# Resident matmul pieces stored with reversed columns and read last to first, in a hybrid decoder layer

## The chip, the cores and the metric

The kernel runs on one core of a Trainium2 chip. Its five engines work side by side, each through its own list of instructions: TensorE (PE, matrix products, with its weight loads shown apart as PEld), VectorE (DVE), ScalarE (ACT), GpSimd (POOL) and SyncE (SP, which here only starts DMAs). The metric is the time on the device in microseconds (us), from launch to end. Beside the runs there is one profiled execution, from which all rows of the profile come.

## The reference

One layer of a decoder is computed for a prompt of 2048 tokens and for 8 x 4 sample tokens, width 1024, all in fp32. After a mixer of recurrent heads come a projection, a cross-attention over 256 memory tokens and a feed-forward part, each with its norms:

```python
def decoder_layer(x, s_gla, s_ssm, conv_buf, mk, mv, lw):
    m, s_gla, s_ssm, conv_buf = mixer(rmsnorm(x, lw['ln_mix_pre']), s_gla, s_ssm, conv_buf, lw)
    h = x + rmsnorm(m, lw['ln_mix_post'])
    a = cross_attend(rmsnorm(h, lw['ln_xa_pre']), mk, mv, lw['w_xq'], lw['w_xo'])
    h = h + rmsnorm(a, lw['ln_xa_post'])
    hf = rmsnorm(h, lw['ln_ffn_pre'])
    f = (jax.nn.silu(hf @ lw['w_gate']) * (hf @ lw['w_up'])) @ lw['w_down']
    h = h + rmsnorm(f, lw['ln_ffn_post'])
    return h, s_gla, s_ssm, conv_buf
```

The mixer ends with a product by `w_out`; the feed-forward width is 2816. The change concerns the products of the prompt from `w_out` on.

## The kernel before

**Two parts.** The first, up to some 838 us, computes the mixer block by block (512 tokens each). The second, which the change touches, runs the large products of the prompt as nine passes: `o` (projection out of the mixer), `s` (scores) and `v` (values), each with 8 units; three passes `g` (gate and up, one for each block of 3, 3 and 2 pairs of token tiles, 22 units each); three passes `d` (down, over 3, 4 and 4 groups of the inner dimension, 8 units each). That is 114 units.

**Products.** A unit is a product of matrices halved in both dimensions, made from seven smaller products in place of eight (the scheme of Strassen and Winograd): sums of quadrants are formed beforehand (`S1` to `S4` and the like), and the seven results are added into four quadrants. In each of the seven, the stationary operand (the weights loaded into TensorE) belongs to the unit and changes with it, and the moving operand stays resident in SBUF for a whole pass. The resident operands of a pass are its seven *pieces*, tiles `r0` to `r6` and, where a piece has four slices of 512 columns, also `e0` to `e6`. A slice is what one matmul streams: 512 columns in the passes `o`, `s`, `v` and `d`; 384, 384 and 272 in the three passes `g`.

**fp32 by three matmuls.** Every operand is split into a high part, rounded to the reduced format fp32r that TensorE takes, and a low part, the rest. `three` (lines 135 to 137) then issues high x high, high x low and low x high into the same bank of PSUM; line 136 takes the low part of the moving operand. The banks of the passes are accA (products 0, 2, 4 and 6 of a unit), accB (product 1) and accC (products 3 and 5).

**How pieces are made.** `pieces_w` (weights) and `pieces_g` (activations) list, for each of the seven pieces, one or more parts. A part's `load(t)` starts a DMA on SP's queue into a staged tile `st` (lines 1778 and 1795) and gives back a view `v` of the staged columns and a function from a resident tile to the place of these columns in it. `Pieces.larger` writes the high part there on ScalarE (line 1739); `smaller` writes staged minus high as the low part (line 1743), on VectorE, or for the second parts of the first `d` pass on GpSimd. The function is applied to the tile of the high part and to that of the low part alike. `Pieces.moving(i, k)` gives the slices that the matmuls of product `i`, step `k` stream.

**Order.** The order of the work is written out by hand: the loop over `order` issues the products of a unit, evacuates its banks, splits the next units' stationary operands (lines 1650, 1668 and 1670) and takes one step of the pieces that come next. The pieces of a pass are made during the last unit of the pass before and its own first unit; before a product's matmuls are issued, the loop completes its piece (`while i not in held[n].full`). `pin` keeps each engine's instructions in the order in which they were traced.

Of the kernel before, what the change touches and what calls it, by code (L numbers as in the profile page):

```python
# [42 lines left out]
def hymba_kernel(ctx: ExitStack, tc: tile.TileContext, a: dict, o: dict, dbg: dict | None = None):  # L43
    nc = tc.nc
# [1656 lines left out]
    class Pieces:  # L1701
# [61 lines left out]

        def moving(self, i, k):
            if self.wide:
                return [r[k // 2][:, k % 2 * 512:(k % 2 + 1) * 512] for r in self.at[i]]
            return [r[:, k * self.w:(k + 1) * self.w] for r in self.at[i]]

    def pieces_w(k, w, t, u0, n):

        wd = lambda h, e: w[h, u0:u0 + n, :, e * 512:(e + 1) * 512].rearrange("u p c -> p u c")
        ts = lambda i: t[i][:, u0:u0 + n]
        srcs = [wd(0, 0), wd(0, 1), ts(1), ts(0), ts(2), wd(1, 1), ts(3)]

        def part(i, k0, k1):
            def load(t):
                v = t[:, 0:(k1 - k0) * 512]
                nc.sync.dma_start(out=v.rearrange("p (k c) -> p k c", c=512), in_=srcs[i][:, k0:k1])
                return v, lambda r: r[k0 // 2] if n == 4 else r[:, k0 * 512:k1 * 512]
            return load  # L1780
        cuts = [(0, 2), (2, n)] if n > 2 else [(0, n)]
        return Pieces(k, [[part(i, *c) for c in cuts] for i in range(7)], 512, 3, n == 4)

    def pieces_g(k, blk):
        js = BLOCKS[blk]
        n = len(js)
        ws = NS // 2 if blk == len(BLOCKS) - 1 else 0
        w = n * P + ws

        by = lambda r: r[:, 0:4 * w].rearrange("p (k w) -> p k w", w=w)  # L1790

        def part(i, n0, n1):
            def load(t):
                v = t[:, 0:(n1 - n0) * 512]
                nc.sync.dma_start(out=v.rearrange("p (j c) -> p j c", c=512), in_=xp[i, js[n0]:js[n0] + n1 - n0].rearrange("j p c -> p j c"))
                return v.rearrange("p (j k c) -> p k j c", k=4, c=P), lambda r: by(r)[:, :, n0 * P:n1 * P].rearrange("p k (j c) -> p k j c", c=P)
            return load

        def sample_part(i):
            def load(t):  # L1800
                v = t[:, 0:4 * ws]
                nc.sync.dma_start(out=v, in_=xps[i])
                return v.rearrange("p (k c) -> p k c", c=ws), lambda r: by(r)[:, :, n * P:w]
            return load
        cuts = [(0, 2), (2, n)] if n > 2 else [(0, n)]
        return Pieces(k, [[part(i, *c) for c in cuts] + ([sample_part(i)] if ws else []) for i in range(7)], w, 3)
# [324 lines left out]
    def pieces_of(k):  # L2131
        kind, i, _ = passes[k]
        if kind == "g":
            return pieces_g(k, i)
        if kind == "d":
            return pieces_w(k, a["w_down"], wT, *PARTS[i])
        return pieces_w(k, *{"o": (a["w_out"], wX[0]), "s": (flat2(wqk), wX[1]), "v": (flat2(wvo), wX[2])}[kind], 0, 4)
# [134 lines left out]
    for e, (n, i) in enumerate(order):  # L2272
        k, g, left = work[n]
        kind, b, gs = passes[k]
        if i == 0:
# [6 lines left out]
            w = now.w  # L2282
# [29 lines left out]
        w = held[n].w  # L2312
# [23 lines left out]
        p = coming if work[cur][2] == 1 else now if begins[cur] else None  # L2336
# [117 lines left out]
```

## Time and profile before

| | |
|---|---|
| median of 3 runs | 2814.31 us (2811.24 to 2816.92) |
| the profiled execution, its own time | 2820.75 us |
| its span, first to last instruction | 2819.0 us |
| mean granted clock of TensorE | 0.991 |
| TensorE busy | 2729.5 us, 97% of the span |
| VectorE busy | 2079.1 us, 74% |
| ScalarE busy | 1472.8 us, 52% |
| GpSimd busy | 536.8 us, 19% |
| moved by DMA | 512.17 MB |

A row of a group of instructions names the line of the kernel, the engine, the operation, the tiles (out<-in), the shape and the count; then busy time in us and the mean of one in ns; then the idle time just before them and what ended it. The chain of waits follows the work that ended last back to the start. TensorE's durations overlap (the next matmul starts before the last one's modelled end), so its pace is read from the starts in the timeline, whose columns are start in us, duration in us, engine and line.

### The profile page before, as it was taken

The numbers are of one execution on the slowest core, as the hardware profiler recorded it, in microseconds if no ns is written. First come the engines' busy times: TensorE is split into PE (matmuls) and PEld (weight loads), VectorE is DVE, ScalarE is ACT, GpSimd is POOL, SyncE is SP. The second block draws the span as 40 slices with busy tenths as digits, with TensorE's granted clock in tenths as the row PEclk, the third lists the DMA queues.
The fourth block names the chain that finished last, engine by engine and source line by source line (L and its number), as shares of the span: only waits on it lengthen the run. The fifth ranks groups of instructions, "written<-read, shape, count | busy, mean of one in ns | idle before, by whom it ended". The sixth has DMA issues, their size and how long they took to land.

```text
span 2819.0 us, 41809 instructions
## 1 busy us (share of the span) xinstructions
PE 2729.5 (97%) x15207; PEld 2367.6 (84%) x15207; DVE 2079.1 (74%) x3831; ACT 1472.8 (52%) x2921; POOL 536.8 (19%) x722
## 2 busy tenths in 40 slices
PE   8999999999998999999899999999999999999998
PEld 8987888788886878878799888899998998788786
DVE  7676677776757787677888787667678878574776
ACT  5545554554546787777755434434445555353432
POOL 2142332321321321015321210001000001000011
PEclk9999999999999999999999999999999999999999
DMA  7345435343266785468864567775234436464765
GB/s 255 113 142 188 148 106 160 118 131 90 83 215 226 282 291 223 146 189 254 263 222 179 177 237 243 253 254 178 98 137 171 156 120 209 168 219 99 239 152 132
DMA packets 151102, 512.17 MB, mean 182 GB/s; under 512 B 18176, under 2 KB 29488, under 8 KB 137328
## 3 DMA queue, kind: packets, MB, share of 16 engines
q1 hardware_dynamic: 94560, 331.81, 36.0%
q0 software_dynamic: 44240, 152.82, 16.8%
q10 hardware_dynamic: 12096, 24.86, 2.7%
q8 instruction: 120, 1.97, 0.3%
q14 instruction: 86, 0.70, 0.1%
HBM read 365.76 MB, written 143.67 MB: 181 GB/s over the span
## 4 chain that ended last, share of the span: by engine, by line
PE 75%; DVE 13%; ACT 5%; DMA 3%; issue 3%; POOL 1%; DVEq 0%; ACTq 0%; SPq 0%; POOLq 0%
PE accA L135 9%; PE accA L136 9%; PE accA L137 9%; PE accC L135 5%; PE accC L136 5%; PE accC L137 5%; PE acc L135 5%; PE acc L136 5%; PE acc L137 5%; PE accB L135 2%; PE accB L137 2%; PE accB L136 2%; DVE s L1670 2%; DVE sum L1650 2%; ACT r L1739 1%
## 5 line engine op out<-in xcount | busy, mean ns | idle before, releaser
L135 PE MATMUL accA<-r,s 128*128 128x512 f32 (+2 forms) x1792 | 637.2, 356 | 19.0 <-ACT r L1739 7.2
L137 PE MATMUL accA<-r,s 128*128 128x512 f32 (+2 forms) x1792 | 629.1, 351 | 2.9 <-DVE s L1670 2.8
L136 PE MATMUL accA<-r,s 128*128 128x384 f32 (+2 forms) x1472 | 502.7, 342 | 2.4 <-DVE r L1743 2.4
L135 PEld LDWEIGHTS accA<-r,s 128*128 128x128 f32 x1792 | 339.2, 189 | 70.9 <-ACT r L1739 11.0
L1668 ACT ACTIVATE s<-sum 128x512 fp32r<-128x512 f32 (+1 forms) x456 | 282.5, 620 | 218.9 <-DVE sum L1650 105.0
L137 PEld LDWEIGHTS accA<-r,s 128*128 128x128 f32 x1792 | 339.7, 190 | 33.2 <-DVE s L1670 4.0
L135 PE MATMUL accC<-r,s 128*128 128x512 f32 (+2 forms) x896 | 318.8, 356 | 9.2 <-ACT s L1668 3.2
L1670 DVE TENSOR_TENSOR s<-sum,s 128x512 fp32r<-128x512 f32 (+1 forms) x456 | 306.8, 679 | 20.1 <-ACT s L1668 19.8
L137 PE MATMUL accC<-r,s 128*128 128x512 f32 (+2 forms) x896 | 314.3, 351 | 0.0
L136 PEld LDWEIGHTS accA<-r,s 128*128 128x128 f32 x1472 | 279.0, 190 | 19.2 <-DVE r L1743 3.6
L1670 DVE TENSOR_TENSOR s<-raw,s 128x512 fp32r<-128x512 f32 (+1 forms) x342 | 233.7, 683 | 52.0 <-ACT s L1668 50.9
L136 PE MATMUL accC<-r,s 128*128 128x384 f32 (+2 forms) x736 | 251.3, 341 | 0.5 <-DVE r L1743 0.5
L1668 ACT ACTIVATE s<-raw 128x512 fp32r<-128x512 f32 (+1 forms) x342 | 213.3, 624 | 72.1 <-PE accC L137 49.8
L129 ACT ACTIVATE whi<-wraw 128x1024 fp32r<-128x1024 f32 (+2 forms) x140 | 128.9, 934 | 184.2 <-PE acc L136 104.5
L135 PEld LDWEIGHTS accC<-r,s 128*128 128x128 f32 x896 | 169.8, 189 | 37.2 <-ACT s L1668 7.8
L130 DVE TENSOR_TENSOR wlo<-wraw,whi 128x1024 fp32r<-128x1024 f32 (+2 forms) x140 | 156.2, 1127 | 48.0 <-ACT whi L129 47.3
L137 PEld LDWEIGHTS accC<-r,s 128*128 128x128 f32 x896 | 169.7, 189 | 14.9 <-DVE s L1670 0.2
L143 POOL TENSOR_TENSOR rs<-ms,nhalf 128x1 f32<-128x1 f32 (+4 forms) x125 | 111.0, 889 | 360.3 <-DVE ms L141 343.9
L135 PE MATMUL acc<-xhl,whi 128*128 128x512 f32 (+1 forms) x464 | 168.1, 363 | 8.3 <-ACT xhl L294 8.2
L137 PE MATMUL acc<-xhl,wlo 128*128 128x512 f32 (+1 forms) x464 | 164.3, 355 | 1.7 <-DVE wlo L130 1.7
L136 PE MATMUL acc<-xhl,whi 128*128 128x512 f32 (+1 forms) x464 | 164.1, 355 | 0.2 <-DVE xhl L295 0.2
L1650 DVE TENSOR_TENSOR sum<-raw 128x512 f32<-128x512 f32 (+1 forms) x228 | 156.4, 686 | 3.6
(696 smaller groups left out, 5857.9 us busy)
## 6 DMA issues: line engine op xcount, KB each, us to landing
raw<-in_w_gu_dram SPq DMA_DIRECT2D x66, 1024.0 KB, 4.9
wraw<-in_w_in_fm_dram SPq DMA_DIRECT2D x52, 512.0 KB, 3.6
wraw<-in_w_in_tm_dram SPq DMA_DIRECT2D x48, 512.0 KB, 3.9
st<-in_w_down_dram SPq DMA_DIRECT2D x37, 512.0 KB, 6.2
aT<-og POOLq DMA_DIRECT2D x22, 768.0 KB, 4.6
raw<-aT SPq DMA_DIRECT2D x16, 1024.0 KB, 6.3
out_y_dram<-y POOLq DMA_DIRECT2D x28, 512.0 KB, 6.1
yp<-y POOLq DMA_DIRECT2D x28, 512.0 KB, 6.6
```

The costliest lines, as they stand in the source:

```text
L129: last[0] = nc.scalar.activation(hi[:, cs], raw[:, cs], AF.Copy)
L130: nc.vector.tensor_tensor(lo[:, cs], raw[:, cs], f(hi)[:, cs], op=ALU.subtract)
L135: nc.tensor.matmul(ps, lhsT=wh, rhs=ah, start=start, stop=False, skip_group_check=more)
L136: nc.tensor.matmul(ps, lhsT=wh, rhs=al, start=False, stop=False, skip_group_check=more)
L137: nc.tensor.matmul(ps, lhsT=wl, rhs=ah, start=False, stop=stop, skip_group_check=more)
L143: nc.gpsimd.tensor_tensor(out=rs[:rows, :cols], in0=ms[:rows, :cols], in1=nhalf[:rows, :cols], op=ALU.pow)
L1650: nc.vector.tensor_tensor(t[out], x, y, op=o)
L1668: nc.scalar.activation(h3, v, AF.Copy)
L1670: return lambda: nc.vector.tensor_tensor(l3, v, f(h3), op=ALU.subtract)
L1739: nc.scalar.activation(hi, v, AF.Copy)
```

## The change

The columns of each slice of a resident piece are stored in reversed order, and the matmuls read the slice from its last address to its first, so that the columns enter TensorE in the order as before and the results stand in natural order. `moving` reverses what it hands out; the functions from a tile to a part's place hand out reversed views, so that lines 1739 and 1743 write (and line 1743 also reads the high part back) downwards. In `pieces_w` the staged view keeps its slices apart, in the shape (128, slices, 512), so that each slice is reversed in itself; the DMA into it is the one of before. In `pieces_g`, `by` reverses each slice of `w` columns, those of the sample tokens included. The stationary operands, the staged tiles and every other instruction stay.

```diff
         def moving(self, i, k):
             if self.wide:
-                return [r[k // 2][:, k % 2 * 512:(k % 2 + 1) * 512] for r in self.at[i]]
-            return [r[:, k * self.w:(k + 1) * self.w] for r in self.at[i]]
+                return [r[k // 2][:, k % 2 * 512:(k % 2 + 1) * 512][:, ::-1] for r in self.at[i]]
+            return [r[:, k * self.w:(k + 1) * self.w][:, ::-1] for r in self.at[i]]
...
                 v = t[:, 0:(k1 - k0) * 512]
-                nc.sync.dma_start(out=v.rearrange("p (k c) -> p k c", c=512), in_=srcs[i][:, k0:k1])
-                return v, lambda r: r[k0 // 2] if n == 4 else r[:, k0 * 512:k1 * 512]
+                v = v.rearrange("p (k c) -> p k c", c=512)
+                nc.sync.dma_start(out=v, in_=srcs[i][:, k0:k1])
+                return v, lambda r: (r[k0 // 2] if n == 4 else r[:, k0 * 512:k1 * 512]).rearrange("p (k c) -> p k c", c=512)[:, :, ::-1]
...
-        by = lambda r: r[:, 0:4 * w].rearrange("p (k w) -> p k w", w=w)
+        by = lambda r: r[:, 0:4 * w].rearrange("p (k w) -> p k w", w=w)[:, :, ::-1]
```

## The prediction

> **What bounds the kernel now.** I read the head of the page first, then the share of each engine and the chain of work that ended last.
>
> ```profile
> span 2819.0 us, 41809 instructions
> ...
> PE 2729.5 (97%) x15207; PEld 2367.6 (84%) x15207; DVE 2079.1 (74%) x3831; ACT 1472.8 (52%) x2921; POOL 536.8 (19%) x722
> ...
> PE 75%; DVE 13%; ACT 5%; DMA 3%; issue 3%; POOL 1%; DVEq 0%; ACTq 0%; SPq 0%; POOLq 0%
> PE accA L135 9%; PE accA L136 9%; PE accA L137 9%; PE accC L135 5%; PE accC L136 5%; PE accC L137 5%; PE acc L135 5%; PE acc L136 5%; PE acc L137 5%; PE accB L135 2%; PE accB L137 2%; PE accB L136 2%; DVE s L1670 2%; DVE sum L1650 2%; ACT r L1739 1%
> ```
>
> TensorE does. Three quarters of the chain are matmuls, and those that write accA, accB and accC (9+9+9+5+5+5+2+2+2 = 48%) take their moving operand from the resident pieces. So the question is almost only: what does one such matmul cost when its moving columns are read from high to low addresses? The groups kept apart by shape count them, and the timeline of TensorE gives their pace, free of the modelled ends: I take starts, not durations.
>
> ```profile
> L135 PE MATMUL accA<-r,s 128*128 128x512 f32 x736 | 293.1, 398 | 9.9 <-DVE y L1850 3.4 <-ACT r L1739 3.4 <-DVE y L2049 1.7
> ...
> L135 PE MATMUL accA<-r,s 128*128 128x384 f32 x704 | 241.3, 343 | 2.5 <-ACT r L1739 1.3 <-ACT s L1668 0.6 <-DVE sg L1981 0.6
> ...
> L135 PE MATMUL accA<-r,s 128*128 128x272 f32 x352 | 102.8, 292 | 6.7 <-DVE t L2002 4.1 <-ACT r L1739 2.5
> ```
>
> Of the seven products of a unit four use accA, two accC and one accB, so all three banks have 7/4 of these counts: 1288, 1232 and 616 on line 135, and the same again on lines 136 and 137. That is 3864 matmuls of 512 columns, 3696 of 384 and 1848 of 272: 9408 matmuls, 3,900,288 columns.
>
> ```profile
> 1102.34 0.40 PE L136 MATMUL accA<-r,s 128*128 128x512 f32 x1
> ...
> 1104.84 0.39 PE L135 MATMUL accB<-r,s 128*128 128x512 f32 x1
> ```
>
> ```profile
> 1600.38 0.33 PE L135 MATMUL accA<-r,s 128*128 128x384 f32 x1
> ...
> 1601.94 0.33 PE L135 MATMUL accA<-r,s 128*128 128x384 f32 x1
> ```
>
> ```profile
> 2199.75 0.29 PE L135 MATMUL accC<-r,s 128*128 128x272 f32 x1
> ...
> 2201.89 0.29 PE L137 MATMUL accA<-r,s 128*128 128x272 f32 x1
> ```
>
> Between the first and the last row lie 11, 9 and 17 starts: 2.50/11 = 0.227 us for 512 columns, 1.56/9 = 0.173 for 384, 2.14/17 = 0.126 for 272. All 9408 take 3864 x 0.227 + 3696 x 0.173 + 1848 x 0.126 = 877 + 639 + 233 = 1749 us of the 1981 us from 838 us (the first piece) to the end. The slope is (0.227 - 0.126)/240 = 0.42 ns for a column; 0.227 us less 512 columns of that leaves 12 ns fixed for each.
>
> **The change, part by part.** No instruction is added, removed or moved. No DMA changes: the staged tiles `st` are filled in natural order as before, by the same issues on SP's queue, so no queue and no wait has anything new in it. The reversed slices cover the same columns of the same tiles. The order in which columns enter TensorE is also unchanged (stored reversed, read reversed), so sums and PSUM writes go as before. Only the direction in which addresses run changes, in three kinds of instruction.
>
> (1) *The moving read of 9408 matmuls.* In none of the matmuls quoted does the moving operand run downwards, so I bound it. Nearest row on the good side: the 0.227 us above, change 0. Nearest on the bad side: columns coming at half the pace, as when the granted clock was low early in the same stage.
>
> ```profile
> 869.53 0.63 PE L137 MATMUL accC<-r,s 128*128 128x512 f32 x1
> ...
> 873.80 0.63 PE L135 MATMUL accA<-r,s 128*128 128x512 f32 x1
> ```
>
> Ten starts lie between them: 0.427 us for 512 columns, 0.834 ns for a column, with no fixed part to be seen. At that pace the columns would take 3,900,288 x 0.834 ns = 3253 us in place of 1749, +1504 us, all on the path, for nothing covers a matmul here. Below nothing: at most the 12 ns fixed, 9408 x 12 ns = -113 us. I take 0. A downward step still moves by one 4-byte word, so neighbours in the stream stay neighbours in memory, and the row just above is only a bound that says what a halved feed would look like.
>
> [...]
>
> (2) *The writes of the high parts (line 1739, ScalarE) and (3) the reads and writes of the low parts (line 1743: VectorE, seven times GpSimd).*
>
> ```profile
> L1739 ACT ACTIVATE r<-st x126: 239/1046/1110, 838.0 to 2673.5; 128x1024 fp32r<-128x1024 f32 x98, 128x512 fp32r<-128x512 f32 x21, 128x64 fp32r<-128x64 f32 x7
> L1743 DVE TENSOR_TENSOR r<-st,r x84: 218/1224/1254, 839.1 to 2670.5; 128x1024 fp32r<-128x1024 f32 x63, 128x512 fp32r<-128x512 f32 x14, 128x64 fp32r<-128x64 f32 x7
> L1743 DVE TENSOR_TENSOR e<-st,r x35: 1216/1225/1226, 841.3 to 2674.6; 128x1024 fp32r<-128x1024 f32 x35
> L1743 POOL TENSOR_TENSOR r<-st,r x7: 1262/1427/1612, 2354.0 to 2384.8; 128x512 fp32r<-128x512 f32 x7
> ```
>
> ```profile
> sum 1981.00, ACT 117.66; mean ACT 9.80
> ```
>
> ```profile
> sum 1981.00, DVE 130.99 POOL 10.09; mean DVE 10.92 POOL 0.84
> ```
>
> The two sums over the stretches from 838 us on, one for each line, say how long they are busy in all. Most lies under matmuls of the pass before; what does not is in the chain of waits after 838 us, whose longest pieces hold 36 of line 1739 (35.6 us in sum) and 31 of line 1743 (36.6 us): 72 us together. The first and the last of the 67:
>
> ```profile
> 838.11 0.97 ACT r L1739
> ...
> 2674.57 1.24 DVE e L1743
> ```
>
> Where they are late TensorE is late next, at the first units of each pass:
>
> ```profile
> PE accA L135 <- ACT r L1739: 7.2, 7, 1.9
> PE accA L136 <- DVE e L1743: 7.2, 8, 1.6
> PE accA L136 <- DVE r L1743: 2.4, 4, 0.8
> ```
>
> [...] Doubled, the chain's 72 us become 144, +72 us, if all of the rest stays hidden; the hidden part would have cover, since ScalarE is busy 52% and VectorE 74%. I take 0 here too, for this reason:
>
> ```profile
> L597 DVE SCALAR_TENSOR_TENSOR xc<-pre,cols,xc 128x512 f32<-128x512 f32 x96 | 71.7, 747 | 1.0
> ...
> L1830 DVE SCALAR_TENSOR_TENSOR y<-y,rs,ga 128x1024 f32<-128x1024 f32 x46 | 58.8, 1277 | 0.6 <-POOL rs L143 0.6
> ...
> L1670 DVE TENSOR_TENSOR s<-sum,s 128x512 fp32r<-128x512 f32 x424 | 288.5, 686 | 17.3 <-ACT s L1668 16.9
> ```
>
> Line 597 reads `pre` shifted by one, two and three words, line 1830 reads whole aligned rows, and the step from 512 to 1024 columns is (1277 - 747)/512 = 1.04 ns a column, against (1224 - 686)/512 = 1.05 for plain subtractions. So a stream that begins off an even word pays nothing in VectorE, and the same is my estimate for one that runs down.
>
> Sum: 0 + 0 + 0. The profiled execution took 2820.75 us (span 2819.0 and 1.75 around it); the median of the runs is 2814.31, 6.44 less. 2820.75 + 0 - 6.44 = 2814 us.
>
> **The rivals.**
>
> *A. The moving read slows when it runs down.* [...] Against it: the step is one word, as before. Price: halved pace +1504 us, 4318 us; a quarter more for each column, 0.105 ns x 3,900,288 = +410 us, 3224 us. It decides from 1.5 ps a column on (5.6 us / 3,900,288).
>
> *B. The pieces are made more slowly.* TensorE's reads are unharmed, but the downward writes and reads of lines 1739 and 1743 take longer, and the starts of the passes stretch. For it: 72 us in the chain and three waits of TensorE in the rows above. Against it: line 597. Price: doubled +72 us, 2886 us; at half of that +36 us, 2850 us; it decides from 8% longer on (5.6/72).
> [...]
>
> *C. The fixed 12 ns of a matmul shrinks,* because its read begins at another end of the slice. Against it: nothing in the rows ties that time to an address; it was not to be seen at the low clock. Price: a tenth of it -11 us, 2803 us; all of it -113 us, 2701 us.
>
> *D. The edit costs waits as well:* slices that run down might be held to overlap more of their tile, so that the second part's high half waits for the first part's low half. Then ScalarE and VectorE alternate where a pass starts: at most the 36.6 us of line 1743 in the chain a second time, 2851 us.
>
> **How the numbers follow.** A measurement of this kernel can tell some 0.2%, 5.6 us, from no change: its runs lie between 2811 and 2817. Chances: forecast 0.52, A 0.20 (half of it or more at the halved pace), B 0.14, D 0.04, C 0.10. Faster is C, 0.10; same is the forecast, 0.52; slower is A, B and D, 0.38. The likeliest case alone lies in 2808 to 2821. The range takes in the smaller C (0.08), the forecast, and B and D up to the doubled price (0.18), 0.78 in all, and reaches a little into A: 2796 to 2900 us. A's larger prices are the part left out.
>
> **What would show it.** Right: starts of 512, 384 and 272 columns still 0.227, 0.173 and 0.126 us apart at full granted clock; line 1739 at 1046 ns and line 1743 at 1224 ns in the median; TensorE's three waits above still near 17 us in sum; the same DMA issues. A: the three spacings grow in proportion to the columns, and the share of TensorE in the chain rises. B: the two medians grow while the spacings stay. C: all three spacings shrink by the same amount. D: the medians stay, and VectorE's and ScalarE's idle time ahead of lines 1739 and 1743 grows. The forecast is wrong if any spacing moves by more than 0.6 ns (5.6 us / 9408).

## The result and the profile after

The changed kernel takes 2845.2 us in the median (2842.57 to 2846.76), the one before 2815.6 us: a ratio of 1.0105, 95% interval 1.0088 to 1.0123. The change costs some 30 us. (One of the four executions of e1_read_only below took 5140.6 us at a granted clock of 0.888, and is left out of its figures.) The profiled execution took 2842.57 us with a span of 2840.9. Head and chain of the page after:

```profile
span 2840.9 us, 41809 instructions
...
PE 2759.4 (97%) x15207; PEld 2377.2 (84%) x15207; DVE 2076.2 (73%) x3831; ACT 1472.3 (52%) x2921; POOL 538.9 (19%) x722
...
PE 71%; DVE 9%; issue 5%; ACT 4%; DMA 3%; POOL 2%; DVEq 0%; POOLq 0%; SPq 0%; ACTq 0%
```

The instructions are the same in number and order. TensorE is busy 30 us longer (2759.4 against 2729.5); VectorE and ScalarE are not. The timeline of TensorE (start and duration in us) says what a matmul takes now: 21 starts for 512 columns, 21 for 384, 17 for 272.

```profile
947.37 0.40 PE L137 MATMUL accA<-r,s 128*128 128x512 f32 x1
...
952.27 0.40 PE L137 MATMUL accB<-r,s 128*128 128x512 f32 x1
```

```profile
1386.54 0.34 PE L135 MATMUL accA<-r,s 128*128 128x384 f32 x1
...
1390.27 0.34 PE L135 MATMUL accC<-r,s 128*128 128x384 f32 x1
```

```profile
2143.42 0.29 PE L135 MATMUL accA<-r,s 128*128 128x272 f32 x1
...
2145.55 0.29 PE L137 MATMUL accC<-r,s 128*128 128x272 f32 x1
```

4.90/21 = 233 ns in place of 227, 3.73/21 = 178 in place of 173, 2.13/17 = 125 in place of 126. Over all back-to-back pairs of the trace the means went from 227.1 to 233.4, from 173.7 to 177.8 and from 126.1 to 125.3 ns. The work on the pieces took as long as before, and TensorE waited no longer for it; the source view of lines 1739 and 1743 and the list of waits say so:

```profile
L1739 ACT ACTIVATE r<-st x126: 239/1044/1105, 836.0 to 2691.6; 128x1024 fp32r<-128x1024 f32 x98, 128x512 fp32r<-128x512 f32 x21, 128x64 fp32r<-128x64 f32 x7
```

```profile
L1743 DVE TENSOR_TENSOR r<-st,r x84: 218/1224/1256, 837.1 to 2688.6; 128x1024 fp32r<-128x1024 f32 x63, 128x512 fp32r<-128x512 f32 x14, 128x64 fp32r<-128x64 f32 x7
L1743 DVE TENSOR_TENSOR e<-st,r x35: 1215/1225/1229, 839.3 to 2692.6; 128x1024 fp32r<-128x1024 f32 x35
L1743 POOL TENSOR_TENSOR r<-st,r x7: 1265/1587/1675, 2367.3 to 2399.1; 128x512 fp32r<-128x512 f32 x7
```

```profile
PE accA L136 <- DVE e L1743: 6.1, 7, 1.6
PE accA L135 <- ACT r L1739: 5.7, 7, 2.0
PE accA L136 <- DVE r L1743: 2.5, 5, 0.8
```

The medians are 1044, 1224 and 1225 ns (before 1046, 1224 and 1225); only GpSimd's seven moved, from 1427 to 1587, 1 us in sum, and not for the direction: with the writes left upward (e1_read_only below) their median is 1587 as well. The three waits sum to 14.3 us, before to 16.8.

### The profile page after: what moved, and what is told of

Read it like the earlier page. It is cut to its first block, busy times and chain, and to the rows that moved or that the text cites. A ratio compares the mean times of both kernels' runs of the same rounds, so it can differ in the third digit from the quotient of the medians.

```text
span 2840.9 us, 41809 instructions
## 1 busy us (share of the span) xinstructions
PE 2759.4 (97%) x15207; PEld 2377.2 (84%) x15207; DVE 2076.2 (73%) x3831; ACT 1472.3 (52%) x2921; POOL 538.9 (19%) x722
## 4 chain that ended last, share of the span: by engine, by line
PE 71%; DVE 9%; issue 5%; ACT 4%; DMA 3%; POOL 2%; DVEq 0%; POOLq 0%; SPq 0%; ACTq 0%
PE accA L135 10%; PE accA L136 9%; PE accA L137 9%; PE accC L135 5%; PE accC L136 5%; PE accC L137 5%; PE acc L135 4%; PE acc L136 4%; PE acc L137 4%; PE accB L135 2%; PE accB L136 2%; PE accB L137 2%; DVE s L1670 1%; ACT r L1739 1%; DVE sum L1650 1%
## 5 line engine op out<-in xcount | busy, mean ns | idle before, releaser
L135 PE MATMUL accA<-r,s 128*128 128x512 f32 (+2 forms) x1792 | 645.9, 360 | 17.4 <-ACT r L1739 5.7
L137 PE MATMUL accA<-r,s 128*128 128x512 f32 (+2 forms) x1792 | 637.2, 356 | 1.8 <-DVE s L1670 1.7
L136 PE MATMUL accA<-r,s 128*128 128x384 f32 (+2 forms) x1472 | 510.5, 347 | 2.5 <-DVE r L1743 2.5
L135 PE MATMUL accC<-r,s 128*128 128x512 f32 (+2 forms) x896 | 323.7, 361 | 7.0 <-ACT sg L1978 3.0
L137 PE MATMUL accC<-r,s 128*128 128x512 f32 (+2 forms) x896 | 318.7, 356 | 0.0
L135 PE MATMUL accB<-r,s 128*128 128x512 f32 (+2 forms) x448 | 159.2, 355 | 0.0
```

What stands on the lines that cost most here:

```text
L135: nc.tensor.matmul(ps, lhsT=wh, rhs=ah, start=start, stop=False, skip_group_check=more)
L136: nc.tensor.matmul(ps, lhsT=wh, rhs=al, start=False, stop=False, skip_group_check=more)
L137: nc.tensor.matmul(ps, lhsT=wl, rhs=ah, start=False, stop=stop, skip_group_check=more)
```

## The experiments

In the first six the edit is in `moving` alone or in the pieces' functions alone; in the other nine, which read a slice block by block, the view of the bank is split into blocks of the same shape as well, in natural order. The distances in the table are means over all back-to-back matmuls of the large passes in each trace (pairs further apart than 1.2 times the median left out). The times are medians for the first four rows and single executions for the rest, beside which the kernel before took 2813.9 to 2817.6 us; the granted clock was 0.991 to 0.996 in all of them.

A word is 4 bytes, one column. By a line the text means an aligned stretch of 64 bytes, 16 words; it is a unit for describing the edits, and no run shows that the memory is built of such lines.

| kernel | what the read does | 512 columns, ns | 384, ns | 272, ns | time, us |
|---|---|---|---|---|---|
| before | upwards, from the start of a 64-byte line | 227.1 | 173.7 | 126.1 | 2815.6 |
| changed | downwards | 233.4 | 177.8 | 125.3 | 2845.2 |
| e1_read_only | downwards, stored as before | 233.4 | 177.8 | 125.3 | 2846.5 |
| e2_write_only | upwards, stored reversed | 227.1 | 173.7 | 126.0 | 2816.1 |
| e3_fwd_plus1 | upwards, one word off | 236.9 | 178.4 | 128.9 | 2860.2 |
| e4_rev_plus1 | downwards, one word off | 236.0 | 178.0 | 127.2 | 2853.4 |
| e8_fwd_plus4 | upwards, four words off | 230.7 | 176.4 | 124.6 | 2828.5 |
| e7_low_only | downwards on line 136 only | 229.1 | 174.7 | 125.5 | 2825.5 |
| e5_blocks16 | 16-word blocks from last to first, upwards inside | 233.4 | 176.7 | 126.4 | 2843.7 |
| e11_blocks32 | 32-word blocks, the same | 232.5 | 175.9 | | 2834.5 |
| e13_blocks64 | 64-word blocks, the same | 227.0 | 173.7 | | 2815.4 |
| e10_blocks128 | 128-word blocks, the same | 227.1 | 173.7 | | 2816.8 |
| e6_inside16 | 16-word blocks upwards, downwards inside | 266.7 | 200.0 | 140.6 | 3044.0 |
| e12_inside128 | 128-word blocks upwards, downwards inside | 233.4 | 177.8 | | 2846.4 |
| e14_swap_pairs | upwards, neighbouring 64-byte lines swapped | 236.0 | 177.8 | | 2855.0 |
| e9_every_other | upwards, every second 64-byte line, then the others | 240.0 | 180.0 | | 2876.2 |
| e15_other128 | upwards, every second 128 bytes, then the others | 236.6 | 176.7 | | 2850.2 |

Where the column of 272 is empty these slices were read as before. The single distances behind a mean can differ: in e9_every_other 237 and 243 ns alternate, in e14_swap_pairs 234 and 239.

### Read or write: e1_read_only and e2_write_only

The theory formed from the two profiles: the downward read of the moving operand costs, by itself (R). The rival is B of the prediction. The first kernel takes the change to `moving` alone, the second everything but that.

```diff
 # e1_read_only: the kernel before, and in moving (both returns alike)
-            return [r[:, k * self.w:(k + 1) * self.w] for r in self.at[i]]
+            return [r[:, k * self.w:(k + 1) * self.w][:, ::-1] for r in self.at[i]]
 # e2_write_only: the changed kernel, and in moving (both returns alike)
-            return [r[:, k * self.w:(k + 1) * self.w][:, ::-1] for r in self.at[i]]
+            return [r[:, k * self.w:(k + 1) * self.w] for r in self.at[i]]
```

> The pieces are stored in natural order as before, and only the matmuls read them last to first, so the columns of each slice come out reversed in the banks and the outputs are not the reference's. Theory R (the downward read itself costs): the starts of 512-column matmuls are 233 ns apart as in the changed kernel, those of 384 about 178, those of 272 unchanged at 125, and the time is that of the changed kernel, 2840 to 2850 us. Rival B (the downward writes of the pieces cost, by making TensorE wait): 227, 173 and 126 ns and 2811 to 2819 us. A mixture would lie between.

> The pieces are stored reversed as in the changed kernel and the matmuls read them first to last as before, so the outputs are not the reference's. Theory R: spacings of 227, 173 and 126 ns and the time of before, 2811 to 2819 us. Rival B: the extra time is here, 2840 to 2850 us, with the spacings of before and longer waits for lines 1739 and 1743.

Measured: e1_read_only 1.0110 times the kernel before (1.0093 to 1.0127), e2_write_only 1.0002 (0.9992 to 1.0011). TensorE's timeline of the one and of the other, 21 starts each:

```profile
2516.56 0.40 PE L137 MATMUL accA<-r,s 128*128 128x512 f32 x1
...
2521.46 0.40 PE L137 MATMUL accC<-r,s 128*128 128x512 f32 x1
```

```profile
2442.08 0.40 PE L137 MATMUL accC<-r,s 128*128 128x512 f32 x1
...
2446.85 0.39 PE L137 MATMUL accA<-r,s 128*128 128x512 f32 x1
```

4.90/21 = 233 ns with the read reversed, 4.77/21 = 227 with only the writes reversed. R holds and B falls: all of the cost is the read.

The two also give the account. The growth in distance times the count is 3864 x 6.3 + 3696 x 4.1 - 1848 x 0.8 = 24.3 + 15.2 - 1.5 = 38 us, of which 29 to 31 us arrive. The stretch from 849 us to the end, for e1_read_only and for e2_write_only:

```profile
sum 1995.00, PE 1934.30; mean PE 1934.30
```

```profile
sum 1966.00, PE 1900.61; mean PE 1900.61
```

TensorE is busy 33.7 us longer and the stretch is 29 us longer, so its idle time fell by 4.7 us (from 65.4 to 60.7). A likely reason, not shown, is that with matmuls that last longer the engines that split operands and empty banks are a little less often late. The other 4 us of the 38 are not attributed either; a part of the matmuls is not back to back or runs at a low granted clock (0.50 from 869.5 to 873.8 us, before, where 512 columns took 427 ns), which the product of count and distance ignores.

### First word or direction: e3_fwd_plus1, e4_rev_plus1 and e8_fwd_plus4

All slices begin at a multiple of 64 bytes (the tiles are placed so, and 512, 384 and 272 columns are whole lines), so a downward read begins at a line's last word. Is it this place, or the direction? A slice is shifted by `up` words, or, where that would leave the written part of the tile, by `down`, which lies at the same place in a 64-byte line.

```diff
-            return [r[:, k * self.w:(k + 1) * self.w] for r in self.at[i]]
+            at = k * self.w
+            at += up if at + self.w + 16 <= min(RW, 4 * self.w) else down
+            return [r[:, at:at + self.w] for r in self.at[i]]
 # e3: up, down = 1, -15; e8: 4, -12; e4: 1, -15 and [:, ::-1]; the wide tiles alike
```

> As before, upwards, but every moving slice is read from one word later (the last slice of a tile from 15 words earlier, which is the same place in a 64-byte line), so the outputs are not the reference's. Theory R1 (a moving read pays for a first word that does not begin a line, whatever the direction; read downwards, the first word is a line's last): 512 columns 233 ns apart, 384 about 178, time 2840 to 2850 us. Theory R2 (it pays for the downward step as such): 227 and 173 ns, 2811 to 2819 us.

> Pieces stored in natural order, slices read last to first as in the changed kernel, but from one word later (the last slice of a tile 15 words earlier), so that the first word read begins a 64-byte line; the outputs are not the reference's. Theory R1: 512 columns 227 ns apart and 384 173, time 2811 to 2819 us. Theory R2: 233 and 178 ns, 2840 to 2850 us. If what counts is how many 64-byte lines a slice touches (here 33 where the changed kernel touches 32): 240 ns, some 2870 us.

> Upwards, every slice read from four words (16 bytes) later, the last slice of a tile from 12 words earlier, which is the same place in a 64-byte line; the outputs are not the reference's. If the read works by lines of 16 bytes the spacings are those of before, 227 and 173 ns, 2811 to 2819 us. If by lines of 64 bytes, those of the shift by one word, 237 and 178 ns, about 2860 us.

Timelines of e3_fwd_plus1 and of e4_rev_plus1, 21 starts each:

```profile
885.75 0.39 PE L137 MATMUL accA<-r,s 128*128 128x512 f32 x1
...
890.72 0.41 PE L137 MATMUL accC<-r,s 128*128 128x512 f32 x1
```

```profile
1060.03 0.40 PE L137 MATMUL accA<-r,s 128*128 128x512 f32 x1
...
1064.99 0.40 PE L137 MATMUL accC<-r,s 128*128 128x512 f32 x1
```

237 and 236 ns. Neither theory had both right. An upward read that begins one word into a line costs more (+9.8 ns) than the aligned downward one (+6.3), so where a slice lies does matter, against R2. But putting the first word of a downward read at the start of a line brought nothing back (236.0), against R1. The two prices do not add up: over an aligned slice the direction costs 6.3 ns, over one shifted by a word nothing more (236.9 upwards, 236.0 downwards). By four words (16 bytes) the shift costs 3.6 ns, neither nothing nor all: neither of the two sizes of a line that were put up.

### Whose price it is: e7_low_only

```diff
 # the wide tiles alike
+                hi, lo = [r[:, k * self.w:(k + 1) * self.w] for r in self.at[i]]
+            return hi, lo[:, ::-1]
```

> Pieces in natural order; only the low parts (line 136, one matmul of three) are read last to first, so one of the three terms has its columns reversed. Theory W (a matmul pays for its own downward read): 233 ns from line 136 to line 137 and 227 after lines 135 and 137 for 512 columns, a third of the extra time, 2823 to 2828 us. Theory T (the turn between an upward and a downward read costs, in the one way or in both): 233 or more on two lines of three, 2835 us or more, or, if only changes of address between neighbours matter, another pattern than one of three.

For 512 columns the distance after line 136 is 232.5 ns, after lines 135 and 137 226.8 and 227.7; the time is 2825.5 us beside 2817.6 of the kernel before. Each matmul pays for its own read (W); the three distances sum to 687.0 ns beside 227.1 + 227.1 + 233.4 = 687.6, so no price for turning between directions shows. For 384 columns the small excess stands after line 137 (176.2) in place of 136 (173.4), so there the attribution to a line is not clean.

### Words or lines: e5_blocks16 and e6_inside16

```diff
+            return [r[:, k * self.w:(k + 1) * self.w].rearrange("p (b c) -> p b c", c=16)[:, ::-1] for r in self.at[i]]
 # e6: [:, :, ::-1]; both: the wide tiles alike, the bank as ps[:, 0:w].rearrange("p (b c) -> p b c", c=16)
```

> Pieces in natural order; each slice is read in blocks of 16 words (64 bytes), the blocks from last to first and the words of a block upwards, so the columns of the results are permuted. Theory I (what costs is that neighbours run down inside a line): 227 ns for 512 columns and 173 for 384, 2811 to 2819 us. Theory O (what costs is that lines come from last to first, so that the next line is never the following one): 233 and 178 ns, 2840 to 2850 us.

> The counterpart: blocks of 16 words from first to last, the words of each block downwards; the columns of the results are permuted. Theory I: 233 ns for 512 columns and 178 for 384, 2840 to 2850 us. Theory O: 227 and 173 ns, 2811 to 2819 us. If every turn from the end of one block to the start of the next costs something, both this one and the blocks in descending order lie above 233 ns.

Timelines of e5_blocks16 and of e6_inside16, 21 starts each:

```profile
851.47 0.40 PE L135 MATMUL accA<-r,s 128*128 128x512 f32 x1
...
856.37 0.40 PE L135 MATMUL accC<-r,s 128*128 128x512 f32 x1
```

```profile
850.92 0.43 PE L135 MATMUL accA<-r,s 128*128 128x512 f32 x1
...
856.52 0.43 PE L135 MATMUL accC<-r,s 128*128 128x512 f32 x1
```

Blocks of 64 bytes from last to first, with the words of each in natural order, cost for 512 columns just what the changed kernel costs, 233 ns, and for 384 three quarters of its extra time (176.7 beside 177.8). So the words need not run down at all; it is enough that the blocks do. The counterpart fits neither theory: 5.60/21 = 267 ns, a quarter over the 213 ns that 512 columns would take at 0.417 ns each (the step between the widths before, (227.1 - 173.7)/128), and 200 ns is a quarter over the 160 of 384. Here every block ends at its low end and the next begins at its high end.

### Which jumps cost: e9 to e15

```diff
 # e9, e15 (c = 16 and 32): every second block of c words, then the others
+            return [r[:, k * self.w:(k + 1) * self.w].rearrange("p (b e c) -> p e b c", e=2, c=16) for r in self.at[i]]
 # e10, e11, e13 (c = 128, 32, 64): blocks from last to first; e12: [:, :, ::-1], c = 128
+            return [r[:, k * self.w:(k + 1) * self.w].rearrange("p (b c) -> p b c", c=128)[:, ::-1] for r in self.at[i]]
 # e14: the two blocks of each pair swapped
+            return [r[:, k * self.w:(k + 1) * self.w].rearrange("p (b e c) -> p b e c", e=2, c=16)[:, :, ::-1] for r in self.at[i]]
 # all: the wide tiles alike; slices of 272 as before; the bank in blocks of the same shape, in natural order
```

> Pieces in natural order; slices of 512 and 384 columns are read upwards, but first every second line of 64 bytes and then the others (those of 272 as before); the columns of the results are permuted. Theory J (every line that is not followed by the next higher one costs a little, whichever way the jump goes): all lines but one jump, 233 ns for 512 columns and about 177 for 384, 2840 to 2850 us. Theory N (only going down costs): 227 and 173 ns, 2811 to 2819 us. Theory F (a read that begins elsewhere than at the lowest line of its slice pays a fixed price): it begins there, 227 and 173 ns.

> Blocks of 128 words (eight lines of 64 bytes) from last to first, upwards inside; slices of 272 as before; the columns of the results are permuted. Theories J and N (a price for each jump): 3 jumps in place of 31, 6.3 x 3/31 = 0.6 ns, so 227 to 228 ns for 512 columns and 173 to 174 for 384, 2813 to 2822 us. Theory F: the full price, 233 and 177 ns, 2840 to 2850 us.

> Blocks of 32 words (two lines) from last to first, upwards inside; slices of 272 as before; the columns of the results are permuted. Theories J and N: 15 jumps in place of 31, 6.3 x 15/31 = 3.0 ns, so 230 ns for 512 columns and about 175 for 384, 2825 to 2835 us. Theory F: 233 and 177 ns, 2840 to 2850 us.

> Blocks of 128 words from first to last, the words of each block downwards; slices of 272 as before; the columns of the results are permuted. The blocks of 16 words of this kind took 267 ns for 512 columns, 40 more than before, 1.25 for each block. If the turn up to the end of the next block is what costs that, four blocks cost 5 ns beside the price of going down inside them, 232 to 238 ns for 512 columns, 2840 to 2865 us. If it is that words run down in a pattern of more than one dimension, 267 ns again, and about 3020 us.

> Blocks of 64 words (256 bytes) from last to first, upwards inside; slices of 272 as before; the columns of the results are permuted. Known: blocks of 16, 32 and 128 words give 233.4, 232.5 and 227.1 ns for 512 columns. Theory 64 (the read works by lines of 64 bytes and each line that is not followed by the next costs): 7 jumps of 31, 227 to 229 ns, 2814 to 2822 us. Theory 128 (it works by pairs of lines, 128 bytes, and order inside a pair is free): 7 jumps of 15, 229 to 231 ns, 2822 to 2832 us. Theory 256 (any jump within reach of 256 bytes costs the same): 232 ns or more.

> Pairs of lines (128 bytes) from first to last, the two lines of each pair swapped, words upwards in each line; slices of 272 as before; the columns of the results are permuted. Theory 128: order inside a pair is free, 227 ns for 512 columns and 173 for 384, 2811 to 2819 us. Theory 64: 31 jumps, among them 15 that skip two lines upwards, 233 to 240 ns, 2840 to 2876 us.

> Upwards, first every second pair of lines (128 bytes), then the others; slices of 272 as before; the columns of the results are permuted. Every second single line took 240 ns for 512 columns and 180 for 384. Theory 64: about half as many jumps and half that price, 233 and 177 ns, 2840 to 2850 us. Theory 128: a pair that is skipped costs what it costs downwards, 232 and 176 ns, 2830 to 2840 us; so only a result at 227 ns (no price for going up) or at 240 (a price for each skip, however long the blocks) tells against both.

Timelines of e9_every_other, e10_blocks128, e13_blocks64 and e14_swap_pairs, 21 starts each:

```profile
1053.42 0.41 PE L135 MATMUL accA<-r,s 128*128 128x512 f32 x1
...
1058.46 0.40 PE L135 MATMUL accA<-r,s 128*128 128x512 f32 x1
```

```profile
1269.21 0.40 PE L136 MATMUL accA<-r,s 128*128 128x512 f32 x1
...
1273.98 0.39 PE L136 MATMUL accB<-e,s 128*128 128x512 f32 x1
```

```profile
2479.73 0.39 PE L136 MATMUL accC<-r,s 128*128 128x512 f32 x1
...
2484.50 0.39 PE L136 MATMUL accA<-r,s 128*128 128x512 f32 x1
```

```profile
2420.84 0.40 PE L136 MATMUL accA<-r,s 128*128 128x512 f32 x1
...
2425.80 0.40 PE L136 MATMUL accA<-r,s 128*128 128x512 f32 x1
```

240, 227, 227 and 236 ns. What follows:

- Going down as such is free where it happens seldom: blocks of 64 or 128 words from last to first cost nothing (227.0 and 227.1), though they begin at the far end. Theory F (a fixed price for beginning elsewhere than at the lowest line) falls.
- Going up with skips costs too, and more: 240 ns. Theory N (only going down costs) falls, unless the pattern itself is to blame, on which more below. J, a price for lines that are not followed by the next higher one, is the one left of the three. It does not cover e3_fwd_plus1 and e6_inside16, where each line is followed by the next and the matmuls still take longer (236.9 and 266.7 ns).
- The price is not so much for each jump. For 512 columns 3 and 7 jumps cost nothing, 15 cost 5.4 ns, 31 cost 6.3 (blocks of 128, 64, 32 and 16 words); 3.0 ns had been expected for 15. So J is wrong in form: there is a step between 7 and 15 jumps, or between blocks of 64 and of 32 words; these runs cannot tell the two apart.
- The two lines of a 128-byte pair are not exchangeable (236 ns with them swapped), so the theory of 128-byte units falls. Theory 64 had the blocks of 64 words and the swapped pairs right, but for every second 128 bytes it gave 233 ns and 236.6 was measured.
- Down inside blocks of 128 words costs 233.4, as over the whole slice; its three turns upwards add nothing. So the 267 ns of e6_inside16 do not come from words running down in blocks as such, but with the turn at every 64 bytes.
- One rival is untested. The reads of e9, e14 and e15 have one level of blocks more than those of the other runs, and no run reads such a pattern in natural order, so a part of their price may be the pattern's own. The 384 columns of e14, at 177.8 ns just as over the whole slice downwards, speak against a large part.

What stays open: the cause of that step; whether the read works in units, and of what size (order matters at 64 bytes in the swapped pairs, 236.0 ns, and, by e6_inside16, 266.7 ns, below that as well when blocks go up); and why slices of 272 columns pay nothing for a downward read (125.3 ns beside 126.1). For the last, the author's guess is the weight loads, which fill nearly all of that pass (PEld is busy 181.4 of the 190 us from 2140 us on, before); no run shows it, and 128.9 ns in e3_fwd_plus1 and 140.6 in e6_inside16 show that a larger price does come through there.

## Why the prediction was wrong

**The forecast.** No change (2814 us, chance 0.52) was the likeliest case, and it did not happen; 2845 us lies inside the range of 2796 to 2900 us but outside the likeliest case's own 2808 to 2821. That it lies in the range is luck: the room above 2821 was made for B and D, neither of which took place, and reached only a little into A.

**The step that failed is term (1) of the sum**, the moving read at 0. It is 38 us by distance and count, and some 30 in the time. The reason given was that a step of one word leaves neighbours in the stream neighbours in memory. That looked at words; the order of blocks of words counts as well, and e5_blocks16 pays the full 6.3 ns (512 columns) with all words of a line in natural order.

**Rival A** named the right operation and the right sign. Its two prices, +410 and +1504 us, were some 14 and 50 times too large: 30 us were measured, and 6.3/512 = 0.012 ns for a column where the smaller price had 0.105. The sentence that it decides from 1.5 ps a column on held. A's chance of 0.20 was put on large prices, half of it or more on the halved pace; a small price for the read, which is what came, had almost no room of its own.

**Rival B** gave 2850 us at half its price, near the result, and for the wrong reason. Terms (2) and (3), 0, were right: with reversed writes alone the ratio is 1.0002 (0.9992 to 1.0011) and the medians on lines 1739 and 1743 stand still on ScalarE and VectorE (1045, 1224 and 1225 ns). No run shows the doubling that B's price of +72 us takes. For VectorE the reading of line 597, a shifted upward read, had pointed that way; for ScalarE the prediction had no row at all, and its 0 was right by luck.

**Rival C** was wrong in sign for 512 and 384 columns, and for 272 what it gained was 0.8 ns. It rightly held that the time beyond the columns' own can hang on the addresses of the read, as e3 to e15 show (227.0 to 266.7 ns for 512 columns), but 227 ns for 512 columns was the least that any of these kernels had as a mean. **Rival D** did not happen: with reversed writes alone the three waits for the pieces sum to 16.8 us (8.2 for line 1739, 8.6 for line 1743), as before.

**The signs to look for** did half of their work. The bound of 0.6 ns for a spacing was exceeded ten times over, and with the medians unchanged that ruled out B. But A's own signs did not come as written: the spacings did not grow in proportion to the columns (+2.8%, +2.4% and -0.6% for 512, 384 and 272), and the share of TensorE in the chain fell from 75% to 71%. That it was the read took e1_read_only and e2_write_only to show.

## What to carry to other kernels

In this kernel, where TensorE is busy 97% of the span, a few ns of a matmul count: 6.3 ns on some four thousand matmuls and 4.1 on as many more made 1%. Let the moving operand begin at a multiple of 64 bytes and run upwards without gaps: 512 columns took 227.1 ns so, 230.7 from 16 bytes later, 236.9 from 4 bytes later and 240.0 with every second 64 bytes first. If it must be read from its end, take blocks of 64 or 128 words from last to first, each upwards, which cost nothing here (227.0 and 227.1 ns), where blocks of 16 and 32 did (233.4 and 232.5). Read the price from the distance between starts of back-to-back matmuls, for each width apart, since the slices of 272 columns here paid nothing for the downward read (125.3 ns beside 126.1).

## What the runs showed of the hardware

- TensorE's moving read, 512 fp32r columns at a mean granted clock of 0.991 to 0.996: 227.1 ns from an address at a multiple of 64 bytes upwards, 230.7 from 16 bytes later, 236.9 from 4 bytes later, 233.4 downwards, up to 266.7 with 64-byte blocks that follow each other upwards and each run down.
- Downward writes of ScalarE and downward reads and writes of VectorE took as long as upward ones (1044 to 1046 and 1224 to 1225 ns in the median, most of them of 1024 columns). GpSimd's seven subtractions took 1587 ns in the median in the changed kernel and 1427 before; but 1587 in e1_read_only too, where they run upwards, so the direction is not the cause.
- Many distances lie 6 to 7 ns apart (227 and 233 ns for 512 columns, 237 and 243 alternating in e9_every_other; 173 and 180 alternating for 384 in e5_blocks16), about 15 columns' worth at 0.417 ns. It is not so everywhere: in e11_blocks32 they spread from 228 to 241. No run was made to explain it.
